# First norm of a two-layer decoder trunk: four of the first half's squares move from ScalarE to GpSimd

## The chip, the cores and the metric

The kernel runs on one core of a Trainium2 chip, so no other core shares its work. The metric is the time of one execution in device microseconds (us), the median of three runs, less is better. In the text TensorE is PE in the rows of the profile (and PEld for its weight loads), VectorE is DVE, ScalarE is ACT, GpSimd is POOL and the engine that issues most loads is SP.

## The reference

The kernel computes a two-layer decoder trunk in float32 for 1024 tokens of width 1024, with 16 meta tokens put ahead of them (1040 in all). Layer 0 has a recurrent branch and a sliding-window attention branch from one input projection, layer 1 is a retention mixer; each is followed by a SwiGLU part. The change touches only the first norm and its neighbour, the first input projection:

```python
def _rmsnorm(x, gain):
    xf = x.astype(F32)
    y = xf * lax.rsqrt(jnp.mean(xf * xf, axis=-1, keepdims=True) + RMS_EPS)
    return (y * gain.astype(F32)).astype(x.dtype)
...
h = jnp.concatenate([meta, x], axis=1)
h = h + _mixer_rglru_swa(_rmsnorm(h, mix_norm_ab[j]), ...)     # begins with h @ w_in
```

So for each of the 1040 tokens the mean of 1024 squares is needed, and one over its root scales that token's row of `h @ w_in`.

## The kernel before

**Layout.** Activations are kept transposed: the width of 1024 lies on 128 partitions in 8 K tiles (`kk` 0 to 7), the tokens lie along the free axis. The tokens are cut into two halves (`hf`): 528 columns (16 meta tokens and 512 tokens) and 512 columns. `load_x` (L317 to L320) loads each K tile of each half into a buffer of its own; the first tile, the first weights, the other seven tiles of the first half, further weights and then the second half's tiles are issued in this order on SP.

**Matrix products.** Every float32 factor is split into a high and a low part, and three matmuls stand for one product: high with high (L160), low with high (L161), high with low (L162). For weights the parts are made by `part`: `hi` on ScalarE (L111), `lo` on VectorE (L113). For the activations of the first norm they are made by `split`: `xh`, the tile times the gain, on ScalarE (L208), and `xl`, what that leaves, on VectorE (L210). For the first half `meta_put` copies the first 16 columns of both parts on GpSimd (L174, L175). The first projection of the first half is 96 matmuls of 264 columns each (two weight blocks, two pieces of 264, eight K tiles, three matmuls); the second half goes in matmuls of 512 columns.

**The norm.** The products use the activations without the norm's factor, and the factor is applied to the product afterwards (`mul` on VectorE in `rnn_in`, seen as L299). `square` adds up the squares over the K tiles in `acc[0]`; it is this function that the change goes around:

```python
def square(ht, kk, hf, acc):                                                       # L214
    ...
    o = NM if hf == 0 else 0
    ps = bank()
    nc.scalar.activation(ps, ht[:, o:n], AF.Square)                                # L221, ScalarE, into PSUM
    nc.vector.tensor_tensor(out=acc[:, o:n], in0=ps, in1=acc[:, o:n], op=ALU.add)  # L222, VectorE
    if o:
        sq = stg.tile([P, NM], F32, tag="sq", bufs=2, name=nm("sq"))
        nc.scalar.activation(sq, ht[:, :o], AF.Square)                             # L225, ScalarE
        nc.gpsimd.tensor_tensor(out=acc[:, :o], in0=acc[:, :o], in1=sq, op=ALU.add)  # L226, GpSimd
```

For the second half the squares are made on ScalarE into one of three buffers `sq` (L337) and added to `acc[1]` on GpSimd (L339). When the eight squares of the first half are summed, `stats` (L233) makes the factor: TensorE sums over the partitions in small matmuls (L241, and L247 for the meta tokens), VectorE scales and adds epsilon (L242, L248), GpSimd takes the power of -1/2 (`pow_mhalf`, L200), VectorE multiplies it into five diagonal matrices (L254, L260), and TensorE spreads these over the partitions (L255, L262), from where ScalarE copies them to `R`. An instruction in float32 can stand in the trace as two passes, so the five of L241 and L247 are ten rows there, and the five of L255 and L262 as well.

**What sets the order.** The text of the program does not set it: a scheduler (the tile framework's, with its own model of the engines' times) orders each engine's instructions, within the data's dependences, when the program is built. Each engine then takes its instructions strictly in that order and waits for data or buffers at the head of its queue. Tile pools give the buffers: `bufs` of them for a tag, the next one is handed out when its last reader is done.

Of the kernel before, what the change touches and what calls it, by code (L numbers as in the profile page):

```python
# [15 lines left out]
F32 = mybir.dt.float32  # L16
F32R = mybir.dt.float32r
AF = mybir.ActivationFunctionType
ALU = mybir.AluOpType
# [3 lines left out]
P = 128  # L23
# [39 lines left out]
def block(b):  # L63

    if b == 0:
        return 0, 0, NM
    t = NM + P * (b - 1)
    return (0, t, P) if b <= 4 else (1, t - 528, P)
# [3 lines left out]
def tile_hybrid(ctx: ExitStack, tc, hT, wfm, wqkv, wo0, lruw, pk, qkg, ck, c0, ret_tab, ret_m,  # L72
                wgu0, wgu1, wd0_0, wd0_1, wd0_2, wd0_3, wd0_4, wd1_0, wd1_1, wd1_2, wd1_3, wr, wro, out):
    nc = tc.nc
# [7 lines left out]
    def nm(s):  # L82
        uid[0] += 1
        return f"{s}{uid[0]}"

    def slot(s, dt=F32):
        return sl.tile([P, W], dt, tag="s", name=nm(s))
# [31 lines left out]
    def unit(src, early=True, eng=nc.vector, pool=None):  # L119
        with tc.high_priority() if early else ExitStack():  # L120
            raw = raw_tile()
            nc.sync.dma_start(raw, src)
            return [part(raw[:, i * 512:(i + 1) * 512], 512, eng, pool if i else None) for i in range(2)]
# [49 lines left out]
    def meta_put(kk, x):  # L173
        nc.gpsimd.tensor_copy(metas[-1][:, kk, :NM], x[0][:, :NM])  # L174
        nc.gpsimd.tensor_copy(metas[-1][:, kk, NM:].rearrange("p (r c) -> p r c", c=NM),  # L175
                              x[1][:, :NM].unsqueeze(1).to_broadcast([P, 2, NM]))
# [27 lines left out]
    def split(ht, kk, hf, gname):  # L204
        n = HN[hf]
        g = par(gname, kk)
        xh = slot("xh", F32R)
        nc.scalar.activation(xh[:, :n], ht[:, :n], AF.Copy, scale=g)  # L208
        xl = slot("xl", F32R)
        nc.vector.scalar_tensor_tensor(out=xl[:, :n], in0=ht[:, :n], scalar=g, in1=f32(xh[:, :n]),  # L210
                                       op0=ALU.mult, op1=ALU.subtract)
        return xh, xl

    def square(ht, kk, hf, acc):  # L214
        n = HN[hf]
        if kk == 0:
            nc.scalar.activation(acc[:, :n], ht[:, :n], AF.Square)
            return
        o = NM if hf == 0 else 0
        ps = bank()  # L220
        nc.scalar.activation(ps, ht[:, o:n], AF.Square)  # L221
        nc.vector.tensor_tensor(out=acc[:, o:n], in0=ps, in1=acc[:, o:n], op=ALU.add)  # L222
        if o:
            sq = stg.tile([P, NM], F32, tag="sq", bufs=2, name=nm("sq"))
            nc.scalar.activation(sq, ht[:, :o], AF.Square)  # L225
            nc.gpsimd.tensor_tensor(out=acc[:, :o], in0=acc[:, :o], in1=sq, op=ALU.add)  # L226
# [6 lines left out]
    def stats(acc, hf, tag):  # L233

        blocks = range(0, 5) if hf == 0 else range(5, 9)
        rc = cp.tile([P, 9], F32, tag=f"rc{hf}", bufs=2, name=nm("rc"))
        big = [b for b in blocks if b > 0]
        ps = bank()
        for b in big:
            _, c, n = block(b)  # L240
            nc.tensor.matmul(ps[:, b:b + 1], acc[:, c:c + n], ones[:, 0:1], start=True, stop=True)  # L241
        nc.vector.tensor_scalar(rc[:, big[0]:big[-1] + 1], ps[:, big[0]:big[-1] + 1], 1.0 / D, EPS,  # L242
                                op0=ALU.mult, op1=ALU.add)
        pow_mhalf(rc[:, big[0]:big[-1] + 1], P, len(big))
        if hf == 0:
            ps = bank()
            nc.tensor.matmul(ps[:NM, 0:1], acc[:, 0:NM], ones[:, 0:1], start=True, stop=True)  # L247
            nc.vector.tensor_scalar(rc[:NM, 0:1], ps[:NM, 0:1], 1.0 / D, EPS, op0=ALU.mult, op1=ALU.add)  # L248
            pow_mhalf(rc[:NM, 0:1], NM, 1)
        R = sl.tile([P, W], F32, tag="R", bufs=3, name=nm("R"))  # L250
        ps = bank()
        for j, b in enumerate(big):
            dg = stg.tile([P, P], F32, tag="dg", bufs=5, name=nm("dg"))
            nc.vector.tensor_scalar(dg, ident, rc[:, b:b + 1], None, op0=ALU.mult)  # L254
            nc.tensor.matmul(ps[:, j * P:(j + 1) * P], ones, dg, start=True, stop=True)  # L255
        o = NM if hf == 0 else 0
        nc.scalar.copy(R[:, o:o + 512], ps)
        if hf == 0:
            dg = stg.tile([P, P], F32, tag="dg", bufs=5, name=nm("dg"))
            nc.vector.tensor_scalar(dg[:NM, :NM], ident[:NM, :NM], rc[:NM, 0:1], None, op0=ALU.mult)  # L260
            ps = bank()
            nc.tensor.matmul(ps[:, :NM], ones[:NM, :], dg[:NM, :NM], start=True, stop=True)  # L262
            nc.scalar.copy(R[:, 0:NM], ps[:, :NM])
        return rc, R
# [33 lines left out]
    def mul(out_, a, b, eng=None):  # L298
        (eng or nc.vector).tensor_tensor(out=out_, in0=a, in1=b, op=ALU.mult)  # L299
# [11 lines left out]
    acc = [slot("acc0"), slot("acc1")]  # L311
# [4 lines left out]
    with tc.tile_pool(name="pre", bufs=1) as pre:  # L316
        def load_x(kk, hf):  # L317
            t = pre.tile([P, HN[hf]], F32, name=f"x{kk}_{hf}")
            nc.sync.dma_start(t, hT[kk, :, H0[hf]:H0[hf] + HN[hf]])
            return t  # L320

        xin = [[load_x(0, 0)], []]
        ux = [unit(wfm[0], False)]
        xin[0] += [load_x(kk, 0) for kk in range(1, KD)]
        nc.sync.dma_start(ckt, ck)
        ux.append(unit(wfm[1], False))
        xin[1] = [load_x(kk, 1) for kk in range(KD)]
        for hf in range(2):
            for kk in range(KD):
                xn[kk][hf] = split(xin[hf][kk], kk, hf, "g0")  # L330
                if hf == 0:
                    meta_put(kk, xn[kk][0])
                if hf == 0:
                    square(xin[0][kk], kk, 0, acc[0])
                else:
                    sq = pre.tile([P, 512], F32, tag="sq", bufs=3, name=nm("sq")) if kk else acc[1][:, :512]
                    nc.scalar.activation(sq, xin[1][kk], AF.Square)  # L337
                    if kk:
                        nc.gpsimd.tensor_tensor(out=acc[1][:, :512], in0=acc[1][:, :512], in1=sq, op=ALU.add)  # L339
            if hf == 0:  # L340
                rc[0], R[0] = stats(acc[0], 0, "m0")
# [14 lines left out]
    with tc.tile_pool(name="m0", bufs=1) as mp:  # L356
# [199 lines left out]
        for grp in (2, 0, 1):  # L556
            us = [unit(wqkv[grp, i], pool=la if i else None) for i in range(2)]
            for b in range(9):
                hf, c, n = block(b)
# [409 lines left out]
    acc = [slot("acc0"), slot("acc1")]  # L969
# [594 lines left out]
```

## Time and profile before

| what | value |
|---|---|
| runs | 2653.93, 2655.24, 2658.02 us (median 2655.24) |
| profiled execution | 2654.91 us, of which span 2653.1 us |
| granted TensorE clock, mean over the span | 0.987 |
| TensorE busy | 2566.4 us (97%), 15782 instructions |
| VectorE busy | 1820.0 us (69%), 3117 instructions |
| ScalarE busy | 1142.6 us (43%), 2416 instructions |
| GpSimd busy | 1468.4 us (55%), 1337 instructions |

The span reaches from the first to the last instruction; what lies around it, 1.8 us, belongs to the execution's own time. Busy is the time in which an engine works on an instruction; an engine that waits at the head of its queue is idle. The granted clock is a share of TensorE's full 2.4 GHz: 0.50 is its lower level of 1.2 GHz.

### The profile page before, as it was taken

The numbers are of one execution on the slowest core, as the hardware profiler recorded it, in microseconds if no ns is written. First come the engines' busy times: TensorE is split into PE (matmuls) and PEld (weight loads), VectorE is DVE, ScalarE is ACT, GpSimd is POOL, SyncE is SP. The second block draws the span as 40 slices with busy tenths as digits, with TensorE's granted clock in tenths as the row PEclk, the third lists the DMA queues.
The fourth block names the chain that finished last, engine by engine and source line by source line (L and its number), as shares of the span: only waits on it lengthen the run. The fifth ranks groups of instructions, "written<-read, shape, count | busy, mean of one in ns | idle before, by whom it ended". The sixth has DMA issues, their size and how long they took to land.

```text
span 2653.1 us, 43334 instructions
## 1 busy us (share of the span) xinstructions
PE 2566.4 (97%) x15782; PEld 2277.6 (86%) x15782; DVE 1820.0 (69%) x3117; ACT 1142.6 (43%) x2416; POOL 1468.4 (55%) x1337
## 2 busy tenths in 40 slices
PE   8988999999999999999999999999999999998999
PEld 7877889999999899888999987777877888886777
DVE  6877686666666879987864445566688555556775
ACT  4665543333333534442233346455543333334442
POOL 3746143555544777456765445455545556555884
PEclk9999999999999999999999999999999999999999
DMA  4011151222223743332222235433332322326442
GB/s 150 22 40 41 53 180 69 105 101 105 91 107 112 249 139 94 119 123 101 96 102 91 97 120 195 148 127 113 116 127 92 111 97 102 107 100 223 147 159 87
DMA packets 145318, 302.32 MB, mean 114 GB/s; under 512 B 18512, under 2 KB 35408, under 8 KB 145104
## 3 DMA queue, kind: packets, MB, share of 16 engines
q1 hardware_dynamic: 103792, 232.49, 26.1%
q10 hardware_dynamic: 41152, 66.54, 6.7%
q8 instruction: 124, 2.03, 0.3%
q14 instruction: 90, 0.74, 0.1%
q0 software_dynamic: 160, 0.52, 0.1%
HBM read 216.60 MB, written 82.89 MB: 113 GB/s over the span
## 4 chain that ended last, share of the span: by engine, by line
PE 80%; DVE 10%; ACT 3%; issue 3%; POOL 2%; DMA 2%; SPq 0%; DVEq 0%; ACTq 0%; POOLq 0%
PE ps L160 16%; PE ps L162 16%; PE ps L161 16%; PE ax L160 9%; PE ax L161 9%; PE ax L162 9%; DVE lo L113 2%; POOL ol L791 1%; DVE ol L791 1%; DVE h L842 1%; DVE xp L770 1%; PE ps L681 1%; DVE T L785 1%; PE ps L1147 1%; DVE qs L299 0%
## 5 line engine op out<-in xcount | busy, mean ns | idle before, releaser
L160 PE MATMUL ps<-oh,hi 128*128 128x260 f32 (+1 forms) x2160 | 690.3, 322 | 20.8 <-ACT oh L790 7.5
L162 PE MATMUL ps<-oh,lo 128*128 128x260 f32 (+1 forms) x2160 | 688.7, 321 | 8.6 <-DVE lo L113 8.3
L161 PE MATMUL ps<-ol,hi 128*128 128x260 f32 (+1 forms) x2160 | 690.6, 321 | 1.5 <-DVE ol L791 0.9
L161 PE MATMUL ax<-ol,hi 128*128 128x260 f32 (+1 forms) x1668 | 536.3, 322 | 2.4 <-DVE ol L791 2.4
L160 PE MATMUL ax<-oh,hi 128*128 128x260 f32 (+1 forms) x1668 | 535.1, 322 | 3.0 <-DVE h L842 1.6
L162 PE MATMUL ax<-oh,lo 128*128 128x260 f32 (+1 forms) x1668 | 532.6, 321 | 0.0
L113 DVE TENSOR_TENSOR lo<-S,hi 128x512 fp32r<-128x512 f32 (+2 forms) x380 | 328.4, 866 | 194.0 <-ACT hi L111 181.1
L160 PEld LDWEIGHTS ps<-oh,hi 128*128 128x128 f32 x2160 | 406.6, 189 | 57.9 <-ACT oh L790 10.8
L111 ACT CAST hi<-S 128x512 fp32r<-128x512 f32 (+2 forms) x380 | 211.2, 559 | 541.4 <-PE ps L161 230.8
L162 PEld LDWEIGHTS ps<-oh,lo 128*128 128x128 f32 x2160 | 406.1, 189 | 43.4 <-DVE lo L113 12.0
L161 PEld LDWEIGHTS ps<-ol,hi 128*128 128x128 f32 x2160 | 408.1, 189 | 34.0 <-DVE ol L791 1.6
L160 PEld LDWEIGHTS ax<-oh,hi 128*128 128x128 f32 x1668 | 315.1, 189 | 30.1 <-ACT hi L111 2.0
L161 PEld LDWEIGHTS ax<-ol,hi 128*128 128x128 f32 x1668 | 315.0, 189 | 28.6 <-DVE ol L791 3.4
L162 PEld LDWEIGHTS ax<-oh,lo 128*128 128x128 f32 x1668 | 314.2, 189 | 25.3 <-DVE lo L113 0.4
L113 DVE TENSOR_TENSOR lo<-raw,hi 128x512 fp32r<-128x512 f32 (+2 forms) x318 | 270.2, 853 | 95.6 <-ACT hi L111 90.4
L299 POOL TENSOR_TENSOR t<-t,rf 128x520 f32<-128x520 f32 (+1 forms) x181 | 267.2, 1484 | 112.5 <-DVE t L1072 48.2
L111 ACT CAST hi<-raw 128x512 fp32r<-128x512 f32 (+2 forms) x350 | 202.1, 585 | 293.4 <-PE ps L161 143.5
L145 POOL TENSOR_TENSOR S<-rb 128x512 f32<-128x512 f32 (+2 forms) x95 | 112.3, 1183 | 307.8 <-DVE lo L113 286.2
L791 POOL TENSOR_TENSOR ol<-raw,oh 128x520 fp32r<-128x520 f32 (+1 forms) x140 | 202.5, 1473 | 33.2 <-ACT oh L790 14.4
L151 POOL TENSOR_TENSOR S<-raw,S 128x512 f32<-128x512 f32 (+2 forms) x95 | 126.8, 1335 | 78.5 <-DVE lo L113 77.0
L146 POOL TENSOR_TENSOR S<-S,raw 128x512 f32<-128x512 f32 (+2 forms) x95 | 112.7, 1186 | 85.7 <-issue 46.3
L149 POOL TENSOR_TENSOR S<-raw,rb 128x512 f32<-128x512 f32 (+2 forms) x95 | 120.7, 1271 | 45.5 <-DVE lo L113 45.5
(306 smaller groups left out, 4772.0 us busy)
## 6 DMA issues: line engine op xcount, KB each, us to landing
raw<-in_wgu_dram SPq DMA_DIRECT2D x50, 512.0 KB, 3.3
raw<-hd SPq DMA_DIRECT2D x77, 260.0 KB, 3.3
raw<-hd SPq DMA_DIRECT2D x77, 256.0 KB, 3.2
rb<-in_wgu_dram SPq DMA_DIRECT2D x38, 512.0 KB, 3.2
raw<-in_wro_dram SPq DMA_DIRECT2D x32, 512.0 KB, 3.3
raw<-in_wr_dram SPq DMA_DIRECT2D x27, 512.0 KB, 3.4
hd<-T ACTq DMA_DIRECT2D x44, 260.0 KB, 2.6
hd<-T ACTq DMA_DIRECT2D x44, 256.0 KB, 3.7
```

The costliest lines, as they stand in the source:

```text
L111: nc.scalar.copy(hi, src)
L113: eng.tensor_tensor(out=lo, in0=src, in1=f32(hi), op=ALU.subtract)
L145: nc.gpsimd.tensor_tensor(out=s1, in0=a21, in1=a22, op=ALU.add)
L146: nc.gpsimd.tensor_tensor(out=s2, in0=s1, in1=a11, op=ALU.subtract)
L149: nc.gpsimd.tensor_tensor(out=s3, in0=a11, in1=a21, op=ALU.subtract)
L151: nc.gpsimd.tensor_tensor(out=s4, in0=a12, in1=s2, op=ALU.subtract)
L160: nc.tensor.matmul(ps, ah, bh, start=first and i == 0, stop=False, skip_group_check=more)
L161: nc.tensor.matmul(ps, ah, bl, start=False, stop=False, skip_group_check=more)
L162: nc.tensor.matmul(ps, al, bh, start=False, stop=last and i == n - 1, skip_group_check=more)
L299: (eng or nc.vector).tensor_tensor(out=out_, in0=a, in1=b, op=ALU.mult)
L681: nc.tensor.matmul(k.po[:n, o:o + 64], sb[:, i * P:(i + 1) * P], vt[:, k.b - len(segs) + 1 + j, g * 64:(g + 1) * 64], start=False, stop=g ...
L791: eng.tensor_tensor(out=lo, in0=src, in1=f32(hi), op=ALU.subtract)
```

## The change

In the first half's loop, for the odd K tiles (1, 3, 5, 7), `square` is no longer called. In its place GpSimd multiplies the whole tile of 128x528 by itself into one of two new buffers (`sq`, tag `sq0`; in the trace this is L299, the line in the helper `mul`), and VectorE adds the result to `acc[0]` (L336). The even K tiles and the second half are computed as before. Lines behind it move by four: the second half's squares are L341, its adds L343.

```diff
@@ -330,7 +330,11 @@
                 xn[kk][hf] = split(xin[hf][kk], kk, hf, "g0")
                 if hf == 0:
                     meta_put(kk, xn[kk][0])
-                if hf == 0:
+                if hf == 0 and kk % 2:
+                    sq = pre.tile([P, 528], F32, tag="sq0", bufs=2, name=nm("sq"))
+                    mul(sq, xin[0][kk], xin[0][kk], nc.gpsimd)
+                    nc.vector.tensor_tensor(out=acc[0][:, :528], in0=acc[0][:, :528], in1=sq, op=ALU.add)
+                elif hf == 0:
                     square(xin[0][kk], kk, 0, acc[0])
                 else:
                     sq = pre.tile([P, 512], F32, tag="sq", bufs=3, name=nm("sq")) if kk else acc[1][:, :512]
```

The scheduler orders the head of the program anew. In the rows below a name such as `xh_186` is a tile with the number of its making, `x_1_117` a K tile of the second half, `x_0_100` one of the first.

On TensorE before, the row sums of the first half's squares stand behind 34 of the 96 matmuls:

```order
L161 MATMUL ps_331<-xl_176,hi_86 128x264
L162 MATMUL ps_331<-xh_174,lo_88 128x264
L161 MATMUL ps_356<-xl_176,hi_86 128x264
L162 MATMUL ps_356<-xh_174,lo_88 128x264
L241 MATMUL ax_223<-ckt,acc_71 128x1 x4
L247 MATMUL ax_230<-ckt,acc_71 16x1
L160 MATMUL ps_331<-xh_186,hi_86 128x264
L160 MATMUL ps_356<-xh_186,hi_86 128x264
```

And now, at the end of the first half's matmuls and the start of the second half's (`ax_423`, 512 columns):

```order
L161 MATMUL ps_394<-xl_203,hi_111 128x264
L162 MATMUL ps_394<-xh_201,lo_113 128x264
L241 MATMUL ax_211<-ckt,acc_71 128x1 x4
L247 MATMUL ax_218<-ckt,acc_71 16x1
L255 MATMUL ax_223<-dg_224,ckt 128x128
L255 MATMUL ax_223<-dg_227,ckt 128x128
L255 MATMUL ax_223<-dg_230,ckt 128x128
L255 MATMUL ax_223<-dg_233,ckt 128x128
L262 MATMUL ax_239<-dg_237,ckt 128x16
L160 MATMUL ax_423<-xh_242,hi_82 128x512
```

The row sums moved from behind 34 matmuls to behind all 96, and the diagonals follow them with no matmul between; before, matmuls of the first half stood between the two.

On GpSimd before, the powers (L200) stand among the copies of the first half:

```order
L174 COPY meta_74<-xh_186 128x16
L175 COPY meta_74<-xl_188 128x32
L174 COPY meta_74<-xh_198 128x16
L200 TENSOR_TENSOR rc_222<-rc_222,mhalf 128x4
L200 TENSOR_TENSOR rc_222<-rc_222,mhalf 16x1
L174 COPY meta_74<-xh_210 128x16
L175 COPY meta_74<-xl_200 128x32
L175 COPY meta_74<-xl_212 128x32
L339 TENSOR_TENSOR acc_72<-acc_72,sq_263 128x512
```

And now:

```order
L174 COPY meta_74<-xh_201 128x16
L175 COPY meta_74<-xl_191 128x32
L175 COPY meta_74<-xl_203 128x32
L343 TENSOR_TENSOR acc_72<-acc_72,sq_251 128x512
L343 TENSOR_TENSOR acc_72<-acc_72,sq_258 128x512
L343 TENSOR_TENSOR acc_72<-acc_72,sq_265 128x512
L343 TENSOR_TENSOR acc_72<-acc_72,sq_272 128x512
L200 TENSOR_TENSOR rc_210<-rc_210,mhalf 128x4
L200 TENSOR_TENSOR rc_210<-rc_210,mhalf 16x1
```

The powers moved behind four adds of the second half's squares.

On VectorE before, around the norm's steps:

```order
L113 TENSOR_TENSOR lo_516<-raw_512,hi_514 128x512
L242 TENSOR_SCALAR rc_222<-ax_223 128x4
L248 TENSOR_SCALAR rc_222<-ax_230 16x1
L113 TENSOR_TENSOR lo_520<-raw_512,hi_518 128x512
L210 SCALAR_TENSOR_TENSOR xl_200<-x_0_100,pkt,xh_198 128x528
L254 TENSOR_SCALAR dg_236<-ckt,rc_222 128x128
```

And now:

```order
L336 TENSOR_TENSOR acc_71<-acc_71,sq_207 128x528
L210 SCALAR_TENSOR_TENSOR xl_249<-x_1_117,pkt,xh_247 128x512
L210 SCALAR_TENSOR_TENSOR xl_256<-x_1_119,pkt,xh_254 128x512
L210 SCALAR_TENSOR_TENSOR xl_263<-x_1_121,pkt,xh_261 128x512
L242 TENSOR_SCALAR rc_210<-ax_211 128x4
L248 TENSOR_SCALAR rc_210<-ax_218 16x1
L210 SCALAR_TENSOR_TENSOR xl_270<-x_1_123,pkt,xh_268 128x512
L210 SCALAR_TENSOR_TENSOR xl_277<-x_1_125,pkt,xh_275 128x512
L210 SCALAR_TENSOR_TENSOR xl_284<-x_1_127,pkt,xh_282 128x512
L254 TENSOR_SCALAR dg_224<-ckt,rc_210 128x128
```

L242 moved behind three low parts of the second half and L254 behind three more. Further back the order is the same from about 60 us on, but for one place on GpSimd near 2430 us, where an L145 of a weight unit stands ahead of an L791 instead of behind it.

## Rows read from the trace of the kernel before

**Rows 1.** The page, busy time by engine, and the chain that ended last.
```profile
PE 2566.4 (97%) x15782; PEld 2277.6 (86%) x15782; DVE 1820.0 (69%) x3117; ACT 1142.6 (43%) x2416; POOL 1468.4 (55%) x1337
...
PE 80%; DVE 10%; ACT 3%; issue 3%; POOL 2%; DMA 2%; SPq 0%; DVEq 0%; ACTq 0%; POOLq 0%
```

**Rows 2.** Stretches: length; busy PE, PEld, DVE, ACT, POOL; clock, DMA, GB/s.
```profile
7.13:14.44 7.31, 5.78 (x24) 4.65 (x24) 7.00 (x11) 7.31 (x20) 2.57 (x13) 0.97 1.03 396
12.00:14.00 2.00, 1.22 (x6) 0.84 (x6) 1.90 (x4) 2.00 (x6) 0.75 (x4) 1.00 1.02 402
14.44:24.20 9.76, 9.76 (x45) 9.61 (x45) 9.18 (x19) 8.91 (x17) 7.35 (x13) 0.50 0.77 265
24.20:30.29 6.09, 6.09 (x49) 5.94 (x49) 2.21 (x4) 1.93 (x5) 5.58 (x3) 0.99 0.01 3
30.29:70.00 39.71, 39.71 (x235) 34.81 (x234) 27.10 (x68) 12.10 (x22) 10.51 (x17) 1.00 0.23 79
```

**Rows 3.** The chain that ended last, in the head: start us, us, what.
```profile
8.24 0.48 ACT ax L221
8.72 0.14 ACT sq L225
```

**Rows 4.** Timeline, TensorE: start us, us, engine, line, operation, tiles, count.
```profile
16.77 0.42 PE L162 MATMUL ps<-xh,lo 128*128 128x264 f32 x1
16.98 1.70 PE L241 MATMUL ax<-ckt,acc 128*128 128x1 f32 x8
...
18.75 0.81 PE L160 MATMUL ps<-xh,hi 128*128 128x264 f32 x2
...
26.68 0.28 PE L160 MATMUL ps<-xh,hi 128*128 128x264 f32 x1
26.80 0.38 PE L255 MATMUL ax<-dg,ckt 128*128 128x128 f32 x2
...
30.29 0.39 PE L160 MATMUL ax<-xh,hi 128*128 128x512 f32 x1
```

**Rows 5.** Timeline, the norm's steps on GpSimd and VectorE.
```profile
18.97 1.53 POOL L200 TENSOR_TENSOR rc<-rc,mhalf 128x4 f32<-128x4 f32 x1 [0.37 <-DVE rc L242]
20.53 0.28 DVE L254 TENSOR_SCALAR dg<-ckt,rc 128x128 f32<-128x128 f32 x1 [0.25 <-POOL rc L200]
```

**Rows 6.** Groups by line and shape: count | busy us, mean ns | idle before.
```profile
L221 ACT ACTIVATE ax<-x 128x512 f32<-128x512 f32 x7 | 4.0, 580 | 0.0
L222 DVE TENSOR_TENSOR acc<-ax,acc 128x512 f32<-128x512 f32 x7 | 4.8, 687 | 0.3
L113 DVE TENSOR_TENSOR lo<-raw,hi 128x512 fp32r<-128x512 f32 x13 | 8.6, 681 | 1.5 <-ACT hi L111 1.5
L299 POOL TENSOR_TENSOR hl<-hl,xc 128x528 f32<-128x528 f32 x4 | 5.3, 1316 | 13.5 <-ACT hl L412 13.5
L339 POOL TENSOR_TENSOR acc<-acc,sq 128x512 f32<-128x512 f32 x7 | 12.0, 1715 | 1.0 <-ACT sq L337 0.6
L210 DVE SCALAR_TENSOR_TENSOR xl<-x,pkt,xh 128x512 fp32r<-128x512 f32 x8 | 9.2, 1191 | 4.3 <-ACT xh L208 4.3
L200 POOL TENSOR_TENSOR rc<-rc,mhalf 128x4 f32<-128x4 f32 x2 | 2.5, 1269 | 4.4 <-DVE t L299 4.1 <-DVE rc L242 0.4
```

**Rows 7.** Timeline, GpSimd, its first two-input add.
```profile
8.30 0.20 POOL L174 CAST meta<-xh 128x16 fp32r<-128x16 f32 x1 [1.17 <-ACT xh L208]
8.94 0.22 POOL L226 TENSOR_TENSOR acc<-acc,sq 128x16 f32<-128x16 f32 x1 [0.44 <-ACT sq L225]
```

**Rows 8.** Timeline, VectorE and GpSimd side by side.
```profile
8.32 0.76 DVE L210 SCALAR_TENSOR_TENSOR xl<-x,pkt,xh 128x528 fp32r<-128x528 f32 x1
...
23.27 3.94 POOL L339 TENSOR_TENSOR acc<-acc,sq 128x512 f32<-128x512 f32 x1
23.34 2.72 DVE L210 SCALAR_TENSOR_TENSOR xl<-x,pkt,xh 128x512 fp32r<-128x512 f32 x4
...
32.34 4.42 DVE L210 SCALAR_TENSOR_TENSOR xl<-x,pkt,xh 128x512 fp32r<-128x512 f32 x2
```

## Prediction

> **What bounds the kernel now.** I read the page first: TensorE is busy for 97% of the span and holds 80% of the chain that ended last [rows 1]. A change in a norm's squares can therefore only matter where TensorE waits for that norm, which is the head of the program, so the next view is the head cut into stretches [rows 2]. Three things are to be seen there. From 7.13 to 14.44 ScalarE is busy all the time (7.31 of 7.31) and VectorE nearly (7.00), while TensorE has gaps: the chain of that stretch runs over ScalarE's `xh` (L208) and its squares (L221, L225) [rows 3]. From 14.44 on TensorE is busy without a gap to the end of the table. And its granted clock is half (1.2 GHz) from about 14.0 to 24.2, after the stretch with gaps, and full (2.4 GHz) again after ten microseconds of work. TensorE leaves the first half's 96 matmuls and starts the 512-column matmuls of the second half at 30.29 [rows 4]; that start is the number I forecast. Behind it TensorE is not idle up to 70 (39.71 of 39.71 [rows 2]), and the transfers there wait for buffers and not for a time of day, so I carry a delay of that start to the end of the kernel one to one.
>
> **What the order changes.** The diff removes little, but the scheduler rewrites the head. Before, the row sums (L241, L247) run at 16.98, in the middle of the matmuls, and 10 us of matmuls pass before TensorE comes to the scaled diagonals (L255, at 26.80) [rows 4]: the chain of norm steps VectorE L242, GpSimd power L200 (at 18.97), VectorE L254 (at 20.53) [rows 5] costs TensorE nothing. After, L241 and L247 stand behind all 96 matmuls, and L255 right behind L247. TensorE takes its queue in order, so the whole chain becomes idle time. On GpSimd the power L200 now has four adds of the second half (now L343) ahead of it; before it had none. On VectorE L242 now has three `xl` of the second half ahead of it and L254 three more.
>
> **The parts, with their costs.**
>
> ScalarE loses four squares of 512 columns and four of 16 columns: the larger ones take 580 ns [rows 6], and on the chain they stand with 0.48 and 0.14 a time [rows 3], so 4 x 0.62 = 2.5 us. They lie on the path up to 14.44 and would let `xh` come 2.5 us sooner.
>
> VectorE swaps four adds from PSUM (L222, 687 ns) for four of 528 columns with both inputs in SBUF (now L336). The nearest row is the two-SBUF-input subtraction L113, 681 ns for 512 columns [rows 6], so 0.70 each and a sum of 0.1 us: nothing by itself.
>
> GpSimd gets four multiplications of 128x528. Undisturbed, the like of it takes 1.32 (L299, mean 1316 ns [rows 6]); it loses four 16-column adds (L226) of 0.22 [rows 7]. So 4 x 1.32 - 4 x 0.22 = +4.4 us on an engine that is busy for 2.57 of the first 7.31 us [rows 2]: room enough by itself.
>
> The price is what the two engines do to one another. The seven GpSimd adds L339 should take 1.28 each (1316 ns x 512/528) and take 1715 ns on average; the `xl` of 512 columns take 0.68 in a run of four (2.72 [rows 8]) and 1191 ns on average [rows 6]. The single cases [rows 8]: the add that starts at 23.27 takes 3.94, which is the time of the four `xl` from 23.34 to 26.06 and then its own 1.28; the two `xl` from 32.34 take 4.42 for 1.4 of work, while GpSimd works on its adds and issues two loads. So one engine stands still while the other runs, for whole instructions, whichever holds its operands first. Before, these cases come from 23.27 on, when TensorE has work in store. After, four GpSimd multiplications fall into the stretch where VectorE has no slack. Per multiplication I take the whole 1.3 us for VectorE; the bounds are 0 (it always slips into VectorE's PSUM adds) and 1.3 plus one displaced `xl`, 2.0.
>
> Walk through the queue. VectorE starts `xl` of K tile 1 at 8.32 as before [rows 8]. Up to the last add of the first norm it has 19 instructions (8 `xl`, 4 `lo`, 3 L222, 4 L336), about 0.65 apart (eleven took 7.00 in the stretch from 7.13 [rows 2]): 12.4 us, so 20.7 without lock-out and 25.9 with 4 x 1.3. TensorE comes to L241 after its 96 matmuls. Before, 34 of them stand ahead of it, so 62 are left at 16.98; 34 at half clock, 0.21 apart (16.77 to 16.98 [rows 4]), last to 24.2, and 28 at 0.12 (26.68 to 26.80 [rows 4]) to 27.6; ScalarE's gift makes that up to 2.5 sooner. Both come to about 26, and L241 and L247 end near 27: their ten small passes took 1.8 at half clock (16.98 to 18.75 [rows 4]) and take about half of that at the full one.
>
> Then the exposed chain, which GpSimd sets. Its four adds start when the copy of the last `xl` is made, at about 25 (24.3 to 27.9, by who wins the lock-outs), and at their mean of 1.72 they end at 32 to 34. L242 comes at 31 to 33: the third `xl` ahead of it needs an `xh` that ScalarE makes only after a square that waits for the first GpSimd add to free its buffer (one of three). The power takes 1.0 to 1.5 (mean 1269 ns [rows 6]): 34.5 to 36. The three `xl` ahead of L254 need ScalarE's `xh`, which again stand behind squares that wait for GpSimd's adds; with L254 of up to 0.28 each [rows 5] the diagonals are made by 36 to 37. L255 and L262 are ten passes of up to 0.19 (two in 0.38 [rows 4]), half of them beside the L254, so I add 1 to 1.5: TensorE starts the second half at 37.0 to 38.5 instead of 30.29, +6.7 to +8.2; I take 37.8, **+7.5 us**.
>
> The clock adds to it. TensorE would stand still from about 27 to 36.5; the one fall that this head shows (to 0.50 in the stretch from 14.44) followed a stretch in which it was busy for 1.22 of 2.00 us [rows 2]. At half clock 264 columns come 0.21 apart and at the full one 0.12 (above), so each microsecond at half clock loses almost half of one. Bounds: 0 (no fall) and 5 (10.2 us of half clock, as from 14.0 to 24.2). All of TensorE's queue is ready when it resumes, so I take 4 us, **+2 us**.
>
> First use of GpSimd's two-input form: at 8.30 a copy starts, the first two-input add follows at 8.94, and the 0.44 idle before it is put down to ScalarE [rows 7]. So a start costs nothing I can see, bounds 0 to 0.44. The Trainium skill, GPSIMD Engine Reference, section Instruction dispatch, says that the first call to a freshly loaded kernel costs about 6 us more, with no visible instruction. By that the first multiplication would end near 14.6 instead of 9, VectorE's sixth instruction would wait for it, and the sum would be about 5 us larger; the row speaks against it.
>
> Far behind, near 2430, GpSimd's order also changes by one place (one L145 moves ahead of one L791, in a program whose order is otherwise the same from about 60 us on): 0, within one GpSimd instruction either way, -1.3 to +1.3.
>
> **Sum:** +7.5 +2 + 0 = +9.5 us. The profiled execution took 2654.91, 0.33 under the median of 2655.24; the three runs reach from 2653.93 to 2658.02. That gives 2664.4 against the profiled execution and 2664.7 by the median; I say 2664.5. A measurement of this kernel can tell about 0.2%, 5.3 us, from no change.
>
> **Rivals.**
>
> *No lock-out in this mix (not slower).* If GpSimd's multiplications always slip in beside VectorE, VectorE ends its part at 20.7, TensorE reaches L241 at 25.1 to 27.6 after its 96 matmuls, the adds on GpSimd are done by then, and only L242, power, L254 and L255 (3.5 to 4 us together) are idle time: second half at 29.3 to 32.3 with L241 and L247, -1 to +2, so 2654 to 2657. For it: the L200 at 18.97 ran beside VectorE at 1.53 and held up nothing [rows 5]. Against it: both single cases of [rows 8]. It decides if the lock-outs in the head sum to under about 2 us. With lock-outs of half the size the start would fall near 34 and the time near 2659, still within 0.2%. Chance 0.25 for both.
>
> *ScalarE's gift arrives and the clock rises early (faster).* The 2.5 us reach TensorE, its gaps of 7 to 14 shrink and the half-clock stretch (10.2 us, of which half is lost) is spared: at best 27 for the second half, -3.2 us, 2651.5. Over 0.2% faster needs two more microseconds from the swap near 2430 or a later fall of the clock that is spared. Chance 0.07.
>
> *More of both (slower still).* Lock-outs of 2.0 each, 4 x 0.7 = +2.8, or half clock for ten microseconds, +3, or both: 2667 to 2670. A late first start of GpSimd, for which no row speaks, is in here with 0.02. Chance 0.12.
>
> *The forecast itself:* 0.56. The chances of slower are then 0.56 + 0.12 = 0.68, within 0.2% 0.25, faster 0.07. The range goes from 2653.5, which takes in nearly all of the rival without lock-outs, to 2670.
>
> **What would show it.** In the changed profile: an idle gap of TensorE of 5 to 10 us between L247 and L255, ended by VectorE's L254; the first 512-column matmul near 38; GpSimd's four L299 of 528 columns at a mean well over 1.32, or VectorE's `xl` of 528 columns well over 0.76; half clock at about 38. ScalarE should show idle time between 8 and 16 where it had none. The forecast is wrong if TensorE's gap is under 3 us, or if the delay at the first 512-column matmul does not come back in the span's end.

## The result and the profile after

The changed kernel takes 2670.63 us in the median of five runs (2663.81 to 2675.65) against 2655.64 of the kernel before: the ratio is 1.0049, with an interval of 1.0035 to 1.0064. Run once more beside the kernel before on one chip it took 2668.35 (six runs, 2663.23 to 2672.32) against 2658.47 (29 runs): 1.0040, interval 1.0026 to 1.0055. The profiled execution took 2670.63, its span 2668.9, which is 15.8 more than the span before.

In stretches, the same as in [rows 2] with a later one added (length; busy PE, PEld, DVE, ACT, POOL; clock, DMA, GB/s), the change shows:

```profile
7.13:14.44 7.31, 5.94 (x22) 5.01 (x23) 7.31 (x8) 6.76 (x15) 7.31 (x9) 1.00 1.03 398
14.44:24.20 9.76, 9.46 (x68) 9.06 (x68) 9.76 (x14) 6.76 (x13) 8.71 (x15) 1.00 0.67 212
24.20:30.29 6.09, 2.40 (x20) 2.08 (x19) 6.09 (x7) 4.72 (x8) 4.57 (x4) 0.98 0.27 89
30.29:40.00 9.71, 5.81 (x16) 4.47 (x17) 8.47 (x16) 0.71 (x2) 7.55 (x11) 0.50 0.17 56
```

VectorE, not ScalarE, is now busy all the time from 7.13 to 30.29 (its busy time is the whole of three stretches; the time that it stands still for GpSimd counts as busy). TensorE loses its time between 24.2 and 40, and the clock's lower level has moved there with it. TensorE's timeline answers to [rows 4]:

```profile
25.73 1.05 PE L241 MATMUL ax<-ckt,acc 128*128 128x1 f32 x8 [0.31 <-DVE acc L336]
26.71 0.20 PE L247 MATMUL ax<-ckt,acc 128*16 128x1 f32 x2
33.63 2.15 PE L255 MATMUL ax<-dg,ckt 128*128 128x128 f32 x6 [6.72 <-DVE dg L254]
36.21 0.80 PE L255 MATMUL ax<-dg,ckt 128*128 128x128 f32 x2 [0.43 <-DVE dg L254]
37.47 0.80 PE L160 MATMUL ax<-xh,hi 128*128 128x512 f32 x1
```

The first 512-column matmul starts at 37.47 instead of 30.29. Between L247 and L255 TensorE is idle for 6.72 us, ended by VectorE's L254. What VectorE and GpSimd do meanwhile answers to [rows 5] and [rows 8] (timeline of the change):

```profile
21.67 6.80 POOL L343 TENSOR_TENSOR acc<-acc,sq 128x512 f32<-128x512 f32 x4
...
25.59 4.09 DVE L210 SCALAR_TENSOR_TENSOR xl<-x,pkt,xh 128x512 fp32r<-128x512 f32 x3
29.61 0.15 DVE L242 TENSOR_SCALAR rc<-ax 128x4 f32<-128x4 f32 x1
...
29.84 2.38 POOL L200 TENSOR_TENSOR rc<-rc,mhalf 128x4 f32<-128x4 f32 x2 [1.36 <-DVE rc L248]
31.73 4.42 DVE L254 TENSOR_SCALAR dg<-ckt,rc 128x128 f32<-128x128 f32 x4
32.19 1.25 POOL L343 TENSOR_TENSOR acc<-acc,sq 128x512 f32<-128x512 f32 x1
33.40 0.75 POOL L367 DMA_DIRECT2D wa<-in_lruw_dram  x1
```

L242 could have started at about 26.9, when the row sums were done, and starts at 29.61, behind three low parts that share the time with GpSimd's adds. The two powers take 2.38. The four L254 take 4.42: the shortest of them takes 0.27, the other three 1.28 to 1.84, and beside these three GpSimd works on a power and an add, on two DMA issues, and on one more add.

VectorE and GpSimd hold one another up from the first multiplication on (timeline of the change, then two groups of it from 7 to 37.5 us, columns as in [rows 6]):

```profile
7.05 2.17 DVE L113 TENSOR_TENSOR lo<-raw,hi 128x512 fp32r<-128x512 f32 x2 [0.25 <-ACT hi L111]
7.11 1.55 POOL L299 TENSOR_TENSOR sq<-x 128x528 f32<-128x528 f32 x1
9.81 1.57 DVE L336 TENSOR_TENSOR acc<-acc,sq 128x528 f32<-128x528 f32 x1
12.26 1.06 POOL L299 TENSOR_TENSOR sq<-x 128x528 f32<-128x528 f32 x1
12.59 1.30 DVE L210 SCALAR_TENSOR_TENSOR xl<-x,pkt,xh 128x528 fp32r<-128x528 f32 x1
15.73 1.46 DVE L210 SCALAR_TENSOR_TENSOR xl<-x,pkt,xh 128x528 fp32r<-128x528 f32 x1
18.41 1.30 DVE L113 TENSOR_TENSOR lo<-raw,hi 128x512 fp32r<-128x512 f32 x2
21.56 2.39 DVE L113 TENSOR_TENSOR lo<-raw,hi 128x512 fp32r<-128x512 f32 x2
23.88 1.79 DVE L336 TENSOR_TENSOR acc<-acc,sq 128x528 f32<-128x528 f32 x1
...
L299 POOL TENSOR_TENSOR sq<-x 128x528 f32<-128x528 f32 x4 | 5.3, 1318 | 0.0
L222 DVE TENSOR_TENSOR acc<-ax,acc 128x512 f32<-128x512 f32 x3 | 2.0, 678 | 0.0
```

The mean of 1318 ns for GpSimd's multiplications hides two kinds: the first two take 1.55 and 1.59, and each begins beside a VectorE instruction with two inputs in SBUF that is already running; the last two take 1.06. On VectorE two L113 take 1.30 undisturbed (at 18.41) and 2.17 beside the first multiplication. The rows fit each engine waiting for the whole of the other's instruction that came first, and then working at its own pace. VectorE's instructions with two inputs in SBUF wait in this way, those with one in PSUM (L222) do not.

**Where the 15.8 us come from.** Four places of the program, the same work in each trace, and the span (the gate matmul is the first of L411, L415 in the change; the score matmuls are the first and the last of L645, L649 in the change):

| kernel | first 512-column matmul | first gate matmul | first score matmul | last score matmul | profiled span |
|---|---|---|---|---|---|
| before, shown ahead | 30.29 | 66.0 | 208.74 | 312.9 | 2653.1 |
| before_again (below) | 29.24 | 65.1 | 207.71 | 318.9 | 2660.4 |
| change | 37.47 | 74.6 | 216.16 | 327.2 | 2668.9 |
| change_again (below) | 38.04 | 75.4 | 218.81 | 323.1 | 2663.4 |

Against the profile shown ahead, the change is 7.2 us late at the second half and 8.6 at the gates, behind the stretch at half clock from 30.29 to 40; at the first scores it is 7.4. Between the first and the last score matmul 6.9 us more appear, most of them in a stretch at half clock behind 258 us that the profile of before does not have. It is taken up under the last experiment. The last 1.5 us come in the long rest of the program.

### The profile page after: what moved, and what is told of

Read it like the earlier page. It is cut to its first block, busy times and chain, and to the rows that moved or that the text cites. A ratio compares the mean times of both kernels' runs of the same rounds, so it can differ in the third digit from the quotient of the medians.

```text
span 2668.9 us, 43317 instructions
## 1 busy us (share of the span) xinstructions
PE 2571.8 (96%) x15782; PEld 2282.4 (86%) x15782; DVE 1825.1 (68%) x3117; ACT 1140.2 (43%) x2408; POOL 1476.2 (55%) x1337
## 4 chain that ended last, share of the span: by engine, by line
PE 80%; DVE 10%; POOL 3%; issue 3%; ACT 2%; DMA 2%; SPq 0%; DVEq 0%; POOLq 0%; ACTq 0%
PE ps L160 16%; PE ps L162 16%; PE ps L161 16%; PE ax L160 9%; PE ax L161 9%; PE ax L162 9%; DVE lo L113 2%; POOL ol L795 1%; PE ps L685 1%; DVE ol L795 1%; DVE h L846 1%; DVE xp L774 1%; DVE T L789 1%; PE ps L1151 1%; DMA h<-keep 1%
## 5 line engine op out<-in xcount | busy, mean ns | idle before, releaser
L113 DVE TENSOR_TENSOR lo<-S,hi 128x512 fp32r<-128x512 f32 (+2 forms) x380 | 329.8, 870 | 195.8 <-ACT hi L111 175.7
L113 DVE TENSOR_TENSOR lo<-raw,hi 128x512 fp32r<-128x512 f32 (+2 forms) x318 | 271.8, 858 | 99.6 <-ACT hi L111 92.0
L299 POOL TENSOR_TENSOR t<-t,rf 128x520 f32<-128x520 f32 (+1 forms) x181 | 268.6, 1492 | 112.5 <-DVE t L1076 49.2
L145 POOL TENSOR_TENSOR S<-rb 128x512 f32<-128x512 f32 (+2 forms) x95 | 112.6, 1186 | 309.5 <-DVE lo L113 288.5
```

What stands on the lines that cost most here:

```text
L113: eng.tensor_tensor(out=lo, in0=src, in1=f32(hi), op=ALU.subtract)
L145: nc.gpsimd.tensor_tensor(out=s1, in0=a21, in1=a22, op=ALU.add)
```

## The experiments

Theory A: the exposed chain of norm steps costs the time in the head, because the scheduler put it behind all 96 matmuls. Theory B: GpSimd's multiplications hold VectorE up, wherever the chain stands. For the stretch far behind, near 258 us, there are rivals of their own, C, C' and D, told with their runs.

### order_only: the changed order without the changed work

```diff
-            if hf == 0:
-                rc[0], R[0] = stats(acc[0], 0, "m0")
...
+                if R[0] is None:
+                    with behind("mm"), behind("xl31"), behind("add4"):
+                        fin = stats_begin(acc[0], 0, "m0")
+                    with behind("xl61"):
+                        rc[0], R[0] = fin[0], fin[1]()
```

`behind` queues what is given out in it behind a named instruction on the same engine: the last of the 96 matmuls, the fourth low part and the fourth add of the second half. Expected:

> The work of before without any change to the squares, but with the norm's steps in the changed order: row sums behind all 96 matmuls, the power behind four adds of the second half, L242 behind three low parts and the diagonals behind three more, the second half's matmuls behind the diagonals. Theory A: the order alone exposes the chain, the first 512-column matmul starts at 33 to 37 instead of 30.29 and the time is 2658 to 2663. Theory B: the order alone costs under 1.5 us, 2654 to 2657.

Measured: 2664.82 (2660.93 to 2671.06) against 2656.84, ratio 1.0032 (1.0022 to 1.0042). Its timeline, where L263 is the diagonals' matmul:

```profile
25.95 0.20 PE L252 MATMUL ax<-ckt,acc 128*16 128x1 f32 x2
31.64 2.15 PE L263 MATMUL ax<-dg,ckt 128*128 128x128 f32 x6 [5.48 <-DVE dg L262]
...
35.47 0.80 PE L160 MATMUL ax<-xh,hi 128*128 128x512 f32 x1
```

No square was moved, and the gap is there: 5.48 against 6.72, the start at 35.47 against 37.47. So the order alone makes 5.2 of the 7.2 us (35.47 - 30.29). Theory B, which gave the order under 1.5, falls for the head. The time is 2 us above what theory A gave: in this profile the clock stands at 0.50 from 260 to 270 us, a stretch like that of the change further back, and the delay, 5.4 at the scores (214.14 - 208.74), is 10.2 at the end.

### power_first: the four adds behind the power

```diff
-                        nc.gpsimd.tensor_tensor(out=acc[1][:, :512], in0=acc[1][:, :512], in1=sq, op=ALU.add)
+                        with tc.issue_after(mark["pow"].ins):
+                            nc.gpsimd.tensor_tensor(out=acc[1][:, :512], in0=acc[1][:, :512], in1=sq, op=ALU.add)
```

> The changed work, with the seven adds of the second half's squares queued on GpSimd behind the norm's power instead of four of them ahead of it. If the four adds ahead of the power are what makes the exposed chain long (theory A), the idle gap of TensorE between L247 and L255 shrinks from 6.72 us to 2 to 4 and the first 512-column matmul starts at 31 to 34 instead of 37.47; time 2656 to 2661 plus later falls of the clock. If the chain is long for VectorE's low parts alone, the start stays at 36 to 38 and the time at 2663 or more.

Measured: 2664.28 (2660.03 to 2676.66), ratio 1.0029 (1.0016 to 1.0041). TensorE's timeline:

```profile
29.72 2.15 PE L255 MATMUL ax<-dg,ckt 128*128 128x128 f32 x6 [3.37 <-DVE dg L254]
...
33.63 0.79 PE L160 MATMUL ax<-xh,hi 128*128 128x512 f32 x1
```

Gap and start lie where they were expected (3.37; 33.63): half of the gap was the GpSimd adds ahead of the power. They cost it by way of VectorE: without them four low parts of 512 columns take 2.73 us (from 23.41), where three took 4.09 in the change, and L242 starts at 26.25 instead of 29.61. The time was missed by 3 us. The clock is at 0.56 from 30 to 40 although the gap is shorter, so eleven of the long matmuls (33.63 to 38.48) still run at the lower level, and at the scores the delay is 5.4 (214.14 - 208.74) instead of 3.3.

### diag_later: the diagonals behind the second half's 48 matmuls

```diff
+                if first:
+                    R[0] = R[0]()
+                    for x, hf, a, b, ps in held:
+                        mul(x[:, 3 + a:3 + b], ps, R[hf][:, a:b])
```

The function that makes the diagonals is now called behind the products of both halves. Expected:

> The changed work, but the diagonals' matmuls and what follows them are given out behind the second half's 48 matmuls of 512 columns instead of ahead of them. Theory A (the exposed chain from L242 to L255 costs the time in the head): TensorE has no idle gap of over 1 us behind L247, the first 512-column matmul starts at 26 to 28 (37.47 in the change, 30.29 before), and the time falls to 2651 to 2657, about that of before or a little under, plus what falls of the clock far behind add (0 or some 6 us in the change). Theory B (GpSimd's multiplications hold VectorE up, wherever the diagonals stand): the second half's matmuls wait for their low parts instead, and the time stays at 2661 or more.

Measured: 2659.67 (2657.24 to 2665.08), ratio 1.0013 (1.0004 to 1.0021). The gap is gone and the start is at 27.30, as theory A has it, but the time is not: my edit made a new wait. The waits of TensorE from 36 to 95 us:

```profile
PE ax L241 <- ACT R L266: 2.7, 1, 2.7
```

The second half's row sums need one of the four PSUM banks that the diagonals hold until ScalarE has copied them, and the diagonals came last of all. With it the clock fell to 0.67 from 40 to 50.

### both_moves and moves_on_before

Both moves together, but the diagonals given out behind the first 24 matmuls of the second half:

```diff
+                late = [(xr[1], 1, 0, 512, proj(us[m], 1, 0, 512, tag="ax")) for m, xr in zip(ms[:1], xrs)]
+                R[0] = R[0]()
+                late += [(xr[1], 1, 0, 512, proj(us[m], 1, 0, 512, tag="ax")) for m, xr in zip(ms[1:], xrs[1:])]
```

> The changed work with both moves together: the second half's adds on GpSimd behind the power, and the diagonals given out behind the first 24 matmuls of the second half (one weight block), so that they neither come too early nor hold the first half's PSUM banks. Theory A (the exposed chain is the whole loss, and the moved squares by themselves help): no gap of TensorE over 1 us behind L247, the first 512-column matmul at 26 to 28, the second half's matmuls done 2 to 4 us sooner than before, time 2652 to 2656, no slower than the kernel before on this chip (2656.8). Theory B (GpSimd's multiplications hold VectorE up in any order): 2659 or more.

Measured: 2653.32 (2651.01 to 2659.49) against 2658.47, ratio 0.9985 (0.9977 to 0.9994): 0.15% faster than the kernel before, 15 us under the change on the same chip. TensorE's timeline:

```profile
26.33 0.20 PE L247 MATMUL ax<-ckt,acc 128*16 128x1 f32 x2
26.46 0.50 PE L160 MATMUL ax<-xh,hi 128*128 128x512 f32 x1
...
34.46 0.36 PE L265 MATMUL ax<-dg,ckt 16*128 16x16 f32 x2 [0.72 <-DVE dg L263]
```

The waits that are left come to 1 us (0.28 and 0.72), with GpSimd's multiplications still at 1318 ns and the low parts of 528 columns at 933. The same two moves on the kernel before:

> The two moves (second half's adds behind the power, diagonals given out among the second half's matmuls) made on the kernel before, without its squares being touched; its row sums stay behind 34 matmuls. If the gain of the kernel with both moves comes from the moves alone, this one gains as much: 0.9977 to 0.9994 of the kernel before, first 512-column matmul at 26 to 29. If it comes from the moved squares, which the two moves only uncover, this one is the same as before within 2 us, its first 512-column matmul at 28 to 30.5.

Measured: 2655.8 (2649.79 to 2659.6) against 2655.34, ratio 1.0000 (0.9992 to 1.0009); start 28.05. So the moves alone gain nothing, which leaves the moved squares as the likely source of some 0.15% once the chain is hidden; the two intervals touch (up to 0.9994, from 0.9992), so it is not shown firmly. One thing more stays open: in both_moves the scheduler also ordered some of the later work differently, in moves_on_before it did not behind the head, and how much of the 0.15% is that was not tried.

### extra_mults: only the multiplications added

```diff
+                if hf == 0 and kk % 2:
+                    sq = pre.tile([P, 528], F32, tag="sq0", bufs=2, name=nm("sq"))
+                    mul(sq, xin[0][kk], xin[0][kk], nc.gpsimd)
                 if hf == 0:
                     square(xin[0][kk], kk, 0, acc[0])
```

> The kernel before with its squares untouched, and four GpSimd multiplications of 128x528 added beside them whose result nobody reads; the row sums still stand behind 34 matmuls. Theory B (the two engines' standing still for one another is what costs the time): VectorE's low parts of 528 columns go from 0.76 to 0.9 or more in the mean, and the first 512-column matmul moves by 3 to 6 us, time 2659 to 2663. Theory A: VectorE is slowed in the same way, but TensorE has matmuls in store, so the start moves by under 2 us and the time is 2655 to 2659.

Measured: 2661.36 (2656.54 to 2667.19), ratio 1.0015 (1.0005 to 1.0026). The groups from 7 to 32 us:

```profile
L210 DVE SCALAR_TENSOR_TENSOR xl<-x,pkt,xh 128x528 fp32r<-128x528 f32 x7 | 6.2, 887 | 0.0
```

The low parts of before in the same stretch:

```profile
L210 DVE SCALAR_TENSOR_TENSOR xl<-x,pkt,xh 128x528 fp32r<-128x528 f32 x7 | 5.3, 759 | 0.0
```

VectorE is slowed much as theory B has it (887 against 759 ns), and the first long matmul starts at 28.49, not later than before. TensorE's store of matmuls swallows most of the slowing; how much can't be read to the microsecond, because the half pace with which TensorE begins (last section) ended at 18.2 here and at 24.3 in before. The time is in theory B's range all the same, but not by way of the head: the first score matmul is at 209.04, 0.3 behind before. In this profile the loss appears behind 2470 us:

```profile
2473.89 12.50 DVE L113 TENSOR_TENSOR lo<-S,hi 128x384 fp32r<-128x384 f32 x1 [1.26 <-ACT hi L111]
2477.91 6.15 POOL L794 TENSOR_TENSOR ol<-raw,oh 128x512 fp32r<-128x512 f32 x5
2488.17 0.80 PE L162 MATMUL ps<-oh,lo 128*128 128x512 f32 x1 [11.92 <-DVE lo L113]
```

One VectorE instruction, which takes 0.54 us undisturbed, takes 12.50, and eleven GpSimd instructions follow one another beside it from 2473.26 to 2485.97 without a pause. TensorE waits 11.92 us for it, the clock is at 0.68 from 2480 to 2500, and the delay goes from 0.6 us at 2403 to 9.6 at 2556. In no other profile does this line take over 2.9 us for one instruction. So the engines' standing still for one another cost the time of this execution after all, but far behind the added multiplications and in one place. Whether the median's 2.9 us come of such cases is left open.

### squares_on_act: the squares back on ScalarE

```diff
-                    mul(sq, xin[0][kk], xin[0][kk], nc.gpsimd)
+                    nc.scalar.activation(sq, xin[0][kk], AF.Square)
```

> The change with the four squares left on ScalarE, in one piece of 528 columns into the new buffers, and VectorE's new adds as in the change; GpSimd gets nothing. The scheduler's order puts the row sums behind 36 matmuls again and the diagonals behind most of the first half. If GpSimd's part is what turned the order (theory A), the first 512-column matmul starts at 28 to 31 and the time is 2653 to 2658, about as before. If the new adds or buffers on VectorE cost the time, 2661 or more.

Measured: 2658.88 (2652.67 to 2663.05), ratio 0.9999 (0.9989 to 1.0009). With GpSimd out of it, the scheduler puts the row sums at 17.02 and the diagonals at 24.36; the long matmuls start at 26.88, sooner than expected, and VectorE's times are the undisturbed ones (from 7 to 32 us):

```profile
L210 DVE SCALAR_TENSOR_TENSOR xl<-x,pkt,xh 128x528 fp32r<-128x528 f32 x8 | 6.0, 759 | 6.0 <-ACT xh L208 6.0
L336 DVE TENSOR_TENSOR acc<-acc,sq 128x528 f32<-128x528 f32 x4 | 2.8, 701 | 0.0
```

The half pace at the start (last section) ended at 16.0 here and at 24.3 in before, which by itself can make the 3.4 us that it is ahead at the second half. They do not reach the end: the waits of TensorE from 36 to 95 us hold one row,

```profile
PE ax L255 <- DVE dg L254: 3.1, 1, 3.1
```

the same chain of the second half's norm, which is late next. At the scores it is 2.4 behind before.

### late_start, change_again, before_again: the stretch near 258 us

The first is the kernel before in its own order, behind a hold:

```diff
-    nc.vector.memset(mhalf, -0.5)
+    for _ in range(140):
+        nc.vector.memset(mhalf, -0.5)
+    tc.strict_bb_all_engine_barrier()
```

> The kernel before, word for word in its order, but everything starts behind a hold of 140 small VectorE writes, some 8 us. For the 6 us that the change loses again near 258 us: theory C, a delay alone moves the program against the clock's falls, so this kernel too shows a stretch at half clock there that before has not, in some of its runs, and the time is spread from 2662 to 2672. Theory D, the fall there comes from the changed work or order: no such stretch here, the time is before plus the hold, 2662 to 2665, with runs as close together as before (4 us).

Measured: 2674.11 (2673.2 to 2683.37), ratio 1.0071. The hold came out at 20.0, not 8: the first matmul starts at 27.13 instead of 7.13. No stretch at half clock follows near 258, and five of the six runs lie within 2.6 us. By its letter this is theory D, on one profile; before_again, below, shows that one profile does not settle it. The 20.0 reach the end nearly whole: 17.6 in the two spans, 17.3 in the medians, 21.2 in the lowest runs.

The change once more:

> The change once more, for its spread beside the kernel before on one chip. Theory C' (8.6 us from the head, and by chance a fall of the clock further back that costs some 6 us): the lowest runs are at 2662 to 2665, others 5 to 12 above, and a profile without such a fall ends 8 to 9 us behind that of before. If the loss near 258 us belongs to the change, every run is at 2668 or more.

Measured: the times given above, lowest 2663.23. In its profile the clock is 1.00 in all four stretches of 5 us from 250 to 270, and its span ends 10.3 behind that of before (2663.4 - 2653.1).

The kernel before once more, unchanged:

> The kernel before, unchanged, for a second profile of its head and of the stretch near 258 us. If the half clock from 14.0 to 24.2 belongs to its work, it is there again and the first 512-column matmul starts at 30.0 to 30.6; if it is chance, the start lies anywhere from 26 to 30, and the head of the change is to be compared with that instead.

Measured: 2662.2 in its one run, 6.9 above the median of the 17 runs of the same kernel beside it. Windows of the kernel before, first the profile shown ahead of the prediction:

```profile
245.00:250.00 5.00, 3.89 (x27) 3.16 (x26) 4.52 (x17) 3.51 (x15) 2.58 (x4) 1.00 0.22 83
250.00:255.00 5.00, 4.92 (x39) 4.29 (x38) 3.81 (x16) 4.12 (x16) 3.86 (x12) 1.00 0.02 3
255.00:260.00 5.00, 4.97 (x40) 4.57 (x40) 3.77 (x14) 3.43 (x16) 2.55 (x8) 1.00 0.34 107
```

then before_again:

```profile
245.00:250.00 5.00, 3.85 (x26) 2.98 (x25) 4.51 (x18) 3.69 (x16) 2.76 (x5) 1.00 0.18 70
250.00:255.00 5.00, 4.94 (x20) 4.19 (x21) 2.83 (x12) 2.88 (x12) 3.67 (x12) 0.57 0.01 3
255.00:260.00 5.00, 5.00 (x25) 5.00 (x26) 1.04 (x5) 1.10 (x3) 0.00 (x0) 0.50 0.00 0
260.00:265.00 5.00, 5.00 (x27) 5.00 (x26) 3.63 (x13) 3.31 (x14) 1.71 (x4) 0.57 0.35 107
```

and the change:

```profile
253.00:258.00 5.00, 3.90 (x28) 3.27 (x28) 4.52 (x17) 3.35 (x14) 2.43 (x4) 1.00 0.22 86
258.00:263.00 5.00, 4.92 (x21) 3.69 (x19) 3.17 (x12) 3.21 (x13) 4.00 (x12) 0.58 0.01 3
263.00:268.00 5.00, 5.00 (x25) 5.00 (x25) 0.79 (x4) 1.10 (x3) 0.00 (x0) 0.50 0.00 0
```

The fall to 1.2 GHz follows the same thinner stretch (3.85 to 3.90 of 5.00 us busy) in one execution of before and in one of the change, and is absent in another of each. From the first to the last score matmul the delay against the profile of before grows by 7.0 us in before_again, by 6.9 in the change, and by 0.1 in change_again, which has no such fall. So it belongs to neither, and theory C' holds: it is chance where it falls. The head's half clock of [rows 2], too, is not recorded in before_again, and its first long matmul starts 1.05 earlier. Whether the change meets such falls more often than the kernel before is not shown. The granted clock over the whole span is 0.981 to 0.987 in the change's eleven runs, 0.984 in the mean, and 0.985 to 0.989 in the 29 runs of before beside change_again, 0.987 in the mean. By estimate that is some 15 us more at half clock, and the stretch from 30 to 40 in the head is 10 of them; before has as much in the head of one profile and none in that of the other.

## Why the prediction was right

The forecast was +9.5 us and 2664.5. The change is slower by 1.0049 and 1.0040 in the two comparisons; on the median of 2655.24 that is 2668.3 and 2665.9. Direction and place came out, and so did the size in the head: 8.6 and 9.4 us at the gates. The first median, 2670.63, stands 0.6 above the range's upper end, by falls of the clock far behind the head, which the prediction had not priced. Several terms of the sum were off in opposite directions, so that it came out is in part luck.

- **The end of the chain.** Forecast 37.8 for the second half's start, measured 37.47 and 38.04. L241 was to start at about 26 (25.73) and L247 to end near 27 (26.91), behind all 96 matmuls. VectorE's last add was to end at 25.9 and ends at 25.67.
- **The lock-out.** The mechanism, that one engine stands still for a whole instruction of the other, is what the rows show. The price, 4 x 1.3 = 5.2 us for VectorE, was too high: beside the four multiplications VectorE loses 2.17 - 1.30, 1.57 - 0.70, 1.30 - 0.76 and 1.46 - 0.76, together 3.0 us. Another 2.2 us, 2.39 - 1.30 and 1.79 - 0.70, are lost beside two of the second half's adds, which the forecast had only behind this point. The sum of 5.2 came out by luck. The multiplication was priced too high as well: the row taken for it reads two different tiles, this one reads one tile twice, and where nothing stands ahead of it it takes 1.06, not 1.32. And in the head the lock-out acted on the time only through the chain: extra_mults has it without a later start.
- **The adds ahead of the power.** This term was laid out wrongly in its parts. They were to start at about 25 and end at 32 to 34; they ran from 21.67 to 28.47, at the expected 1.70 each. L242 came at 29.61, not 31 to 33.
- **The power and the diagonals** were mis-sized the other way: the power was taken at 1.0 to 1.5 and the two of them took 2.38; four L254 of up to 0.28 each took 4.42. The two errors cancelled. That the adds do cost is shown by power_first, 3.8 us of start.
- **ScalarE's gift of 2.5 us** reaches ScalarE: its last `xh` of the first half ends at 16.08 (14.74 + 1.34), before at 19.50 (18.78 + 0.72), and it has idle time from 7 to 24 (busy for 6.76 of 7.31 and 6.76 of 9.76). That it reaches TensorE is not shown. The second half starts at 26.46 in both_moves and at 28.05 in moves_on_before, but the half pace at the start ended at 18.7 in the one and at 22.6 in the other, and by estimate this alone makes 1.8 us.
- **The clock** was put at +2. Half clock does stand from 30.29 to 40, and the delay grows from 7.2 at the second half's start to 8.6 at the gates, and in the second profile from 7.8 to 9.4: 1.4 and 1.6.
- **First use of GpSimd's form:** the Trainium skill (GPSIMD Engine Reference, Instruction dispatch) would have had the first multiplication some 6 us longer. It ran from 7.11 for 1.55, as long as the second with 1.59. The trace shows no such price here, whether it does not apply to this form or had been paid before, and the row that I had trusted held.
- **One to one to the end:** late_start's 20.0 arrive as 17.6 in the spans, so near enough; but the end also carries chance falls of some 6 us, which I had not priced, though the runs of before reach 4 us apart already.
- **The swap near 2430** is of no account: change_again stands 10.5 behind at 2400 and 10.3 at the end.

## What to carry to other kernels

A small change of engine can make a scheduler move a whole dependence chain; compare the orders first, and ask of each moved wait what work still stands between it and its engine's next use. Moving work off a busy engine pays only if what it feeds stays covered: here the same squares cost 0.4 to 0.5% with the chain exposed, and with two moves in the order that hid it the kernel was 0.15% faster than before. Before a difference far from the change is explained, profile the kernel before a second time.

## What was not expected of the hardware

- VectorE and GpSimd wait for one another by whole instructions when both read from SBUF, and it goes both ways. VectorE's addition of 528 columns takes 0.70 us or 1.57 and 1.79; GpSimd's multiplication takes 1.06 or 1.55 and 1.59; VectorE's adds from PSUM keep their 0.68. The engine that waits does not always come next: in extra_mults one VectorE instruction took 12.50 us beside eleven GpSimd instructions in a row.
- TensorE starts at half pace with a granted clock of 1.00 in the records. Matmuls of 264 columns come 0.22 us apart first and 0.12 apart later: in the change from 16.5 on, in before_again from 22.0 on, both recorded at 1.00 all along. In before they come 0.22 apart up to 11.4, 0.12 apart for a short time, and from 14.0 to 24.3 0.22 again, now with 0.50 recorded. So the recorded clock does not show this beginning, and its end lies between 16.0 and 24.3 in the profiles (late_start, which begins 20 us later, aside). By estimate from the two spacings each microsecond of it costs TensorE 0.45, so starts in the head can differ by up to 3.7 us for this alone. The idle gaps from which the chain was read are not touched by it. What sets its end was not tried.
